# Loading the first tile sooner and doing mixer A's time-step projection during the merge: a two-layer hybrid decoder trunk on eight cores

## The chip, the cores and the metric

The kernel runs on all eight cores of one Trainium2 chip. Each core does one of the eight batch elements, so the cores do the same work and don't talk to each other. The metric is the device time of the slowest core in microseconds (us). A core has five engines that run in parallel: PE (TensorE, matmuls), DVE (VectorE), ACT (ScalarE), POOL (GpSimd) and SP (SyncE). The DMA engines move data and are started from the queues of SP, ACT and POOL.

A program on all eight cores has two states. In the fast one all cores hold nearly the full TensorE clock. In the slow one the cores of one die, or of both, show a lower granted clock in the records. A ratio below is the mean time of one kernel's fast runs over the mean of the other's of the same rounds, so it is not quite the ratio of the medians quoted beside it. Because few runs are wholly fast, I use a second measure too, called the **core mean**: the mean span of all cores that sit on an undisturbed die (granted clock above 0.985), over all runs of a kernel, with its standard error. It takes the mean of the cores where the metric takes the slowest, so it is some 20 us lower; between groups of runs I compare only the differences from the kernel before of the same group.

## The reference

```python
def hybrid_layer(x, pos, c_act, w_ada, b_ada, w_in, ...):      # cut and condensed
    shift, scale, gate = split(c_act @ w_ada + b_ada)          # each (B, 2048)
    h    = x * (1 + scale) + shift
    proj = h @ w_in                                            # one combined projection
    (a_z, a_xbc, a_dt, b_q, ..., merge) = split(proj)
    ys = (ssd_branch(a_z, a_xbc, a_dt, ...),                   # mixer A: Mamba-2
          swa_branch(...), shortconv_branch(...), rglru_branch(...))   # mixers B, C, D
    m   = sum_k sigmoid(merge_k + b_gate_k) * (ys[k] @ w_branch[k])
    return layer_norm(alpha * x + gate * (m @ w_out), ln_w, ln_b)

def ssd_branch(z, xbc, dt, ...):                               # mixer A, cut
    dt  = softplus(dt + dt_bias)                               # (B, L, 16 heads)
    da  = dt * -exp(a_log)
    cum = cumsum(da, within chunks of 128 tokens)              # the cumulated decay
    ...                                                        # exp(cum_l - cum_s) weights the chunk
```

There are 8 batch elements of 2048 tokens, 2048 channels and two layers. The inputs are random, not zeros.

## The kernel before

Each layer is done in two halves of 1024 tokens, and a half as two tiles of 512 (`ti` = 0, 1). A half has a projection and mixer stage (mixers A to D), a merge stage of 16 steps of 41.5 us, an output stage of 16 products, and layer norm. From one half to the next there is a **boundary**; the program has three. Every operation is recorded with a priority `P.key`; a list scheduler then fixes each engine's order, and semaphores are set where one operation needs another.

The head of the program computes the conditioning of the first two thirds (`shift`, `scale`): 32 weight pieces of 1 MB are multiplied by c on DVE. Then x is loaded and h is made from it:

```python
    P.key = -2.0                                     # c: after all the weights
    P.dma("sp", CACT, c_in, writes=[rCACT], nbytes=8192)
    ...
    P.key = -100.0
    for b4 in range(4):
        for blk in (b4, 4 + b4):
            ...
            ada_piece(0, blk, kc, 4, acc_t, slot, "sp" if np_ % 2 == 0 else "act", [rGO] if np_ == 22 else [])
    ...
    P.key = -50.0
    for kc in range(NKC):
        make_h(0, 0, kc, WS1 if kc % 2 else WS2)     # x in the projection weights' buffers
```

While half n is merged, the h of half n+1 is made and stored to HBM, then loaded when the merge is over:

```python
    def pre_h(n, kc):                                # called once per merge step
        w, rw = WS1.get()
        P.dma("sp", xt, src[kc, :, ...], reads=..., writes=[rw], ...)
        for ti in range(NU):
            b, rb = BB.get()                         # 8 buffers of bf16 512
            act(b, xt[...], AF.Identity, ...)        # ScalarE makes h
            P.dma("sp", hs[n, ti][...], b, reads=[rb], writes=[rHS[n][kc]], ...)
            BB.put((b, rb))
        WS1.put((w, rw))
```

At a boundary, mixer A's small "dt chain" is done for each tile of 512 tokens by itself, with that tile's new h:

```python
    def dt_a(l, u, ti):
        pb, rpb = PX.get()                           # PX: three PSUM banks, also mixer A's transposes
        for v in range(4):
            mms([(pb[:, v*16:(v+1)*16], HT[ti][:, kc, v*128:(v+1)*128], WDT[:, kc, :], ...) for kc in range(NKC)], ...)
        tt(dtt, pb[:, 0:64], dt_bias, ALU.add, ...)  # reads the bank: 128x64
        PX.put((pb, rpb))
        softplus(...); ...                           # some ten more operations of 128x64
        mms([... "triu", ... "ones" ...]); ...       # cumulated sums
        act(f[0:16, 0:T], pb[0:16, :], AF.Copy, ...)
        P.dma("act", cumd[s]..., f..., ...)          # the decay to HBM; mixer A reads it back broadcast
```

In mixer A, `P.dma("act", cu, cumd[...].partition_broadcast(128))` is that broadcast read, and the ScalarE operations that use it follow on the same in-order queue.

The softmax here doesn't subtract the row's maximum and nothing guards it: scores larger than these inputs give would overflow.

## Time and profile before

| what | number |
|---|---|
| recorded time, median of 6 runs (lowest to highest) | 6867.13 us (6399.38 to 7307.74) |
| the two fast ones of the six | 6399.38 and 6410.06 us |
| fast mean in the four later groups of runs | 6390.7, 6393.9, 6394.9, 6392.1 us |
| profiled execution: slowest core, mean granted clock | 6409.0 us, 0.990 to 0.992 on all cores |
| dense matmuls start | 172.6 us |
| PE's longest wait at the three boundaries | 16.0, 12.0, 7.5 us |

In all views "PE" without idle time in front of it is the good case: the matmuls set the time, and a microsecond in which PE is idle is a microsecond of the total. What PE waited for is therefore the first thing to read. In a line of a timeline, `ps<-arena` says what was written from what (`ps` is PSUM, the banks that PE writes its products to, `arena` the other on-chip memory), and the bracket gives the idle time before it and what ended it.

### The profile page before, as it was taken

The page shows a single profiled execution, that of the slowest core. Times are in us where ns is not written, and L with a number is a line of the kernel's source. Part 1 is how long each engine was busy: PE and PEld are TensorE (multiplying, and loading weights), DVE is VectorE, ACT ScalarE, POOL GpSimd, SP SyncE. Part 2 cuts the span into 40 slices and gives each one's busy share as a digit, 9 for nine tenths or more (in the row PEclk, how much of TensorE's full clock was granted, in tenths as well). Part 3 has the DMA queues.
Part 4 walks back from the last instruction along what each step waited for, and adds up shares of the span by engine and source line. Part 5 has one row for each costly group of instructions (what it writes and reads, how often), then busy time and mean ns, then how long its engine had stood idle before and what let it go on. Part 6 is the DMA issues. An engine that isn't in the chain of part 4 may idle for free.

```text
span 6409.0 us, 91209 instructions; the slowest of 8 cores (6371.9 to 6409.0 us)
## 1 busy us (share of the span) xinstructions
PE 6062.2 (95%) x31047; PEld 2900.4 (45%) x31644; DVE 3457.1 (54%) x6217; ACT 2193.1 (34%) x4123; POOL 580.9 (9%) x1044
## 2 busy tenths in 40 slices
PE   1999999999999999999999999999999999999998
PEld 0444444444444444444444444444444444444445
DVE  5676664344687665432377776322247766622225
ACT  1555541111355453121135555311114545511113
POOL 0111000000001000000000110000000000000004
PEclk9999999999999999999999999999999999999999
DMA  9877668788687766784579776755557776544445
GB/s 281 128 126 129 123 117 181 153 177 197 137 145 126 120 116 125 172 176 77 127 138 144 120 130 117 159 89 90 90 147 139 137 121 120 112 73 76 77 74 149
DMA packets 281833, 838.53 MB, mean 131 GB/s; under 512 B 35488, under 2 KB 63264, under 8 KB 276768
## 3 DMA queue, kind: packets, MB, share of 16 engines
q0 software_dynamic: 134944, 503.51, 49.2%
q1 hardware_dynamic: 100224, 247.05, 13.2%
q10 hardware_dynamic: 46208, 82.09, 5.7%
q8 instruction: 261, 4.28, 0.3%
q14 instruction: 196, 1.61, 0.1%
HBM read 1264.39 MB, written 65.27 MB: 207 GB/s over the span
## 4 chain that ended last, share of the span: by engine, by line
PE 85%; DMA 7%; issue 2%; ACT 2%; DVE 2%; ACTq 1%; SPq 0%; DVEq 0%; POOL 0%; POOLq 0%
PE ps L486 84%; DMA arena<-cum_scr 2%; ACT arena L458 2%; DMA arena<-x_scr 1%; ACTq L275 1%; DVE arena L462 1%; PE ps L491 1%; DVE arena L466 1%; DMA arena<-arena 1%; DMA arena<-wg 1%; DMA cum_scr<-arena 1%; DMA arena<-w 1%; DMA arena<-w_ada 0%; SPq L275 0%; DMA arena<-cp 0%
## 5 line engine op out<-in xcount | busy, mean ns | idle before, releaser
L486 PE MATMUL ps<-arena 128*128 128x512 bf16 (+6 forms) x30407 | 6038.2, 357 | 291.6 <-DVE arena L466 147.7
L486 PEld LDWEIGHTS ps<-arena 128*128 128x128 bf16 (+3 forms) x31004 | 2846.4, 101 | 3387.5 <-issue 464.4
L466 DVE SCALAR_TENSOR_TENSOR arena<-arena,ps 128x512 f32<-128x512 f32 (+1 forms) x832 | 570.8, 690 | 1718.1 <-PE ps L486 1432.1
L458 ACT ACTIVATE arena<-arena 128x512 f32<-128x512 f32 (+11 forms) x2360 | 1108.0, 518 | 1124.8 <-DVE arena L466 426.0
L462 DVE TENSOR_TENSOR arena<-arena 128x512 f32<-128x512 f32 (+7 forms) x2054 | 1231.0, 618 | 337.7 <-ACT arena L458 158.9
L458 ACT ACTIVATE arena<-ps,arena 128x512 f32<-128x512 f32 x648 | 443.8, 687 | 2166.3 <-PE ps L486 2152.7
L466 DVE SCALAR_TENSOR_TENSOR arena<-arena 128x512 f32<-128x512 f32 (+2 forms) x1281 | 920.6, 734 | 351.5 <-ACT arena L458 208.8
L458 ACT ACTIVATE arena<-ps 128x512 f32<-128x512 f32 (+3 forms) x949 | 535.8, 580 | 813.3 <-PE ps L486 651.6
L275 POOL DMA_DIRECT2D arena<-w x544 | 289.5, 532 | 3185.9 <-PE ps L486 2821.6
L462 DVE TENSOR_TENSOR arena<-ps,arena 128x4 f32<-128x4 f32 (+5 forms) x936 | 330.2, 374 | 234.1 <-PE ps L486 152.1
L275 POOL DMA_DIRECT2D arena<-wg x384 | 204.3, 532 | 2313.8 <-PE ps L486 2312.6
L466 DVE SCALAR_TENSOR_TENSOR arena<-ps,arena 128x512 f32<-128x512 f32 (+3 forms) x153 | 104.1, 680 | 164.2 <-PE ps L486 145.1
L462 DVE TENSOR_TENSOR ps<-ps,arena 128x512 f32<-128x512 f32 (+1 forms) x225 | 148.5, 663 | 13.8 <-DVE arena L466 0.5
L491 PE MATMUL ps<-arena 128*128 128x128 bf16 (+1 forms) x640 | 102.6, 250 | 43.2 <-DVE arena L462 42.0
L491 PEld LDWEIGHTS ps<-arena 128*128 128x128 bf16 (+1 forms) x640 | 64.6, 116 | 108.4 <-issue 62.1
L458 ACT ACT_TABLE_LOAD x64 | 82.1, 1283 | 64.6 <-DMA arena<-c 40.6
L462 DVE TENSOR_TENSOR arena<-arena,ps 128x256 f32<-128x256 f32 (+1 forms) x178 | 78.5, 451 | 31.4 <-PE ps L486 26.7
L1061 DVE TENSOR_TENSOR_SCAN arena<-arena 128x512 f32<-128x512 f32 x64 | 80.9, 1264 | 0.5
L477 DVE RECIPROCAL arena<-arena 128x4 f32<-128x4 f32 (+2 forms) x145 | 69.4, 479 | 16.6 <-ACT arena L458 11.0
L472 DVE TENSOR_SCALAR arena<-arena 128x512 bf16<-128x512 f32 (+6 forms) x211 | 66.7, 334 | 20.8 <-DMA arena<-w_ada 10.7
L1211 POOL TENSOR_TENSOR arena<-arena 128x256 f32<-128x256 f32 (+1 forms) x45 | 41.0, 912 | 82.0 <-ACT arena L458 81.7
L1047 ACT ACT_TABLE_LOAD x32 | 41.1, 1283 | 16.1 <-issue 13.4
(24 smaller groups left out, 127.7 us busy)
## 6 DMA issues: line engine op xcount, KB each, us to landing
arena<-w POOLq DMA_DIRECT2D x544, 512.0 KB, 6.4
arena<-wg POOLq DMA_DIRECT2D x384, 512.0 KB, 6.9
arena<-w_ada SPq DMA_DIRECT2D x128, 512.0 KB, 10.6
arena<-cum_scr ACTq DMA_DIRECT2D x128, 256.0 KB, 6.2
arena<-wo_scr SPq DMA_DIRECT2D x64, 512.0 KB, 4.7
arena<-arena ACTq DMA_DIRECT2D x352, 64.0 KB, 4.9
arena<-w_ada ACTq DMA_DIRECT2D x16, 1024.0 KB, 11.0
arena<-w_ada SPq DMA_DIRECT2D x16, 1024.0 KB, 9.8
```

Source lines behind the costliest of these rows:

```text
L275: eng.dma_start(out=o.fn[0], in_=o.fn[1]).then_inc(s, 16)
L458: P.op("act", lambda e: e.activation(out=out, in_=in_, func=func, **kw), reads, writes, cost=c_act(n) + (0.09 if bias is not None and not ...
L462: P.op(eng, lambda e: e.tensor_tensor(out=out, in0=in0, in1=in1, op=op), reads, writes, cost=c_dve(n * (0.5 if fast else 1.0)), acc=acc)
L466: P.op("dve", lambda e: e.scalar_tensor_tensor(out=out, in0=in0, scalar=scalar, in1=in1, op0=op0, op1=op1), reads, writes, cost=c_dve(n) + ...
L472: return e.tensor_scalar(out=out, in0=in0, scalar1=s1, scalar2=None, op0=op0)
L477: P.op("dve", lambda e: e.reciprocal(out=out, in_=in_), reads, writes, cost=0.1 + n * 6.3e-3)
L486: r = e.matmul(out, lhsT=lhsT, rhs=rhs, start=st, stop=sp_, skip_group_check=True)
L491: P.op("pe", lambda e: e.transpose(out=out, in_=in_, identity=ident), reads, writes, cost=cost, acc=acc)
L1047: r = e.activation(out=cv[:, 0:T], in_=cv[:, 0:T], func=AF.Sqrt, scale=-1.0, bias=ko("quarter"))
L1061: P.op("dve", lambda e, cv=cv, a=a, xs=xs, init=init: e.tensor_tensor_scan(out=cv[:, 0:T], data0=a[:, 0:T], data1=xs[:, 0:T], initial=init ...
L1211: P.op("pool", lambda e, s2=s2, f=f: e.tensor_tensor(out=s2, in0=s2, in1=f, op=ALU.add), [rf, rs2], [rs2], cost=0.16 + n * 2.2e-3)
```

## The change

The intent is to start dense matmuls earlier and to take the dt chain off the boundaries. In the head: c first, all conditioning weights on SyncE's queue and contiguous in HBM, x for the first tile between them in its own buffers, x for the second tile on GpSimd's queue, and two projections before the dt chain. At the boundaries: the dt product is accumulated in the merge stage, block by block of h, and one chain for both tiles follows.

```diff
-    P.key = -2.0
+    P.key = -200.0
     P.dma("sp", CACT, c_in, writes=[rCACT], nbytes=8192)
...
-        P.dma(q, w[:, 0:nk * 512], w_ada[l, blk][:, kc * 512:(kc + nk) * 512], ...)
+        P.dma(q, w[:, 0:nk * 512], w_ada[l, blk, kc // 4][:, (kc % 4) * 512:(kc % 4 + nk) * 512], ...)
...
-    def pre_h(n, kc):
+    def pre_h(n, kc, bank):
...
             act(b, xt[:, ti * T:(ti + 1) * T], AF.Identity, ...)
+            mms([(bank[0][:, (4 * ti + v) * 16:(4 * ti + v + 1) * 16], b[:, v * 128:(v + 1) * 128], WDT[:, kc, :], False,
+                  kc == NKC - 1) for v in range(4)], [rb, rWDT], [bank[1]], 4 * 0.06, acc=True)
             P.dma("sp", hs[n, ti][:, kc * T:(kc + 1) * T], b, ...)
             BB.put((b, rb))
...
+    def dt_chain(l, u, tis, bank, pool):        # the body of the old dt_a, over 128 columns for two tiles
...
-        if u == 0:
+        if n == 0:
             layer_consts(l)
+            load_wdt(l)
+        for col in (A_X, A_Z) if n == 0 else ():
+            wt = load1(WS1, l, col, n)
+            pre[col] = proj(0, wt, PX), PX
+            WS1.put(wt)
-        for ti in range(NU):
+        for ti in range(NU) if n == 0 else ():
             dt_a(l, u, ti)
...
+        if n < 3:                                # before the merge stage
+            bank = PX.get()
+            P.op("dve", lambda e: e.memset(bank[0][:, 0:64 * NU], 0.0), ...)
...
-            sums.append((PX.get(), PX.get() if ti == 0 else PM.get()))
+        sums = [(PX.get(), PX.get()), (PM.get(), PM.get())]
...                                              # after the output stage and layer norm
+        P.key = k0 + UL
+        dt_chain((n + 1) // 2, (n + 1) % 2, list(range(NU)), bank, F2)
+        PX.put(bank)
...
-                ada_piece(0, blk, kc, 4, acc_t, slot, "sp" if np_ % 2 == 0 else "act", [rGO] if np_ == 22 else [])
+                ada_piece(0, blk, kc, 4, acc_t, slot, "sp", rGO if np_ == 29 else [])
...
+        for kc in range(4 * b4, 4 * b4 + 4):     # inside the loop over the four groups of weights
+            x, rx = F.get()
+            P.dma("sp", x[:, 0:T], x_in[kc, :, 0:T], writes=[rx], nbytes=262144)
+            first_h(0, kc, x[:, 0:T], rx)
+            F.put((x, rx))
+    for b4 in range(4):
+        P.key = 20.5 + 10.2 * b4
+        x, rx = ring.get()
+        P.dma("pool", ..., x_in[4 * b4:4 * b4 + 4, :, T:2 * T]..., writes=[rx], nbytes=1048576)
...
-    P.key = -50.0
-    for kc in range(NKC):
-        make_h(0, 0, kc, WS1 if kc % 2 else WS2)
```

## The prediction

> **What bounds the kernel now.** I read the cores first: the eight spans of the profiled execution lie between 6371.9 and 6409.0 us at a granted clock of 0.990 to 0.992 on both dies, so it is an undisturbed, fast one. The six times on record run from 6399 to 7308 us; the two lowest, 6399.38 and 6410.06, agree with each other and with this profile, and the others are slow-state runs. All my numbers, the predicted time too, are for the fast state, with 6405 us (the mean of those two) as "before".
>
> Then the page. Busy time with its share and instruction count, and the strips in 40 slices of 160 us:
>
> ```profile
> PE 6062.2 (95%) x31047; PEld 2900.4 (45%) x31644; DVE 3457.1 (54%) x6217; ACT 2193.1 (34%) x4123; POOL 580.9 (9%) x1044
> ...
> PE   1999999999999999999999999999999999999998
> ...
> DMA  9877668788687766784579776755557776544445
> ```
>
> PE is the bound everywhere but in the first slice, where the DMA engines are. All there is to win without removing matmuls is PE's idle time, 6409 - 6062 = 347 us, and this change removes no large matmul. So I asked who PE waited for (total us, times, longest):
>
> ```profile
> PE ps L486 <- DVE arena L466: 147.7, 13, 64.4
> PE ps L486 <- DVE arena L462: 58.1, 45, 5.0
> PE ps L491 <- DVE arena L462: 42.0, 8, 16.0
> ```
>
> The first line is the head; L491 is the transpose of mixer A, of which single waits reach 16 us. I looked at each place in turn. The head by windows (PE, PEld, DVE, ACT, POOL busy; granted clock; DMA share; GB/s):
>
> ```profile
> 0.00:40.00 40.00, 0.00 (x0) 0.00 (x0) 0.12 (x3) 0.00 (x0) 3.83 (x8) 1.00 0.92 283
> 40.00:80.00 40.00, 3.54 (x16) 3.48 (x16) 33.88 (x76) 8.01 (x15) 0.00 (x0) 1.00 0.76 252
> 80.00:120.00 40.00, 3.68 (x16) 3.56 (x16) 24.91 (x46) 5.76 (x8) 0.00 (x0) 1.00 0.97 321
> 120.00:160.00 40.00, 13.52 (x56) 8.85 (x58) 33.45 (x53) 5.76 (x8) 2.13 (x4) 1.00 0.98 268
> 160.00:200.00 40.00, 36.06 (x225) 17.90 (x227) 17.81 (x45) 15.70 (x30) 5.83 (x11) 0.96 0.82 131
> ```
>
> and by the timeline:
>
> ```profile
> 18.49 3.31 SPq L275 DMA_DIRECT2D arena<-c  x1
> ...
> 40.56 1.28 ACT L458 ACT_TABLE_LOAD   x1 [40.56 <-DMA arena<-c]
> ...
> 138.49 0.54 POOL L275 DMA_DIRECT2D arena<-w  x1 [133.81 <-ACT arena L458]
> ...
> 172.59 17.64 PE L486 MATMUL ps<-arena 128*128 128x512 bf16 x77 [0.23 <-issue]
> ```
>
> The 8 KB tensor c, which every conditioning product needs, is issued at 18.5 us behind ten megabytes of weights and x, and lands at 40.6: VectorE does nothing until then. Meanwhile its weight ring is full, so the DMA share falls to 0.76 in the next window. The first projection weight is issued at 138.5 us, because its buffers carry x until ScalarE has made h. Dense matmuls begin at 172.6.
>
> The other place is the boundary from one half of a layer to the next. The chain that ended last, near the first of them:
>
> ```profile
> 1731.11 8.65 DMA cum_scr<-arena
> ...
> 1740.23 18.95 DMA arena<-cum_scr
> ```
>
> and PE's timeline there:
>
> ```profile
> 1763.60 0.59 PE L491 MATMUL ps<-arena 128*128 128x128 bf16 x4 [15.99 <-DVE arena L462]
> 1763.98 3.62 PE L486 MATMUL ps<-arena 128*128 128x512 bf16 x8
> ```
>
> The dt chain of mixer A (small matmuls, about twenty tiny vector operations, a write of the cumulated decay to HBM, a broadcast read of it) only starts when the new h is there; ScalarE waits for the read at the head of its queue, then DVE, then PE, for 16.0 us. At the second boundary the same wait is 12.0 us, at the third 7.5.
>
> **What the Trainium skill says.** (1) "DMA: Bandwidth & Descriptors", Specifications, gives about 358 GB/s of HBM to a core. The trace agrees in kind: 321 GB/s over 80 to 120 us at a share of 0.97. The head is a bandwidth problem, and only bytes moved out of it or idle DMA time can shorten it. (2) Same page, Queues, rings and completion order: an SDMA engine takes its queue rows in turn, packet by packet. So weights on GpSimd's queue will take a share from conditioning weights still under way on SyncE's. No view before isolates this. (3) "TensorE: Matmul & The Clock Gate", Part 1: the array falls to half clock when idle for a window of about 3.4 us and takes about as long to recover. The trace agrees: the 8 matmuls after the 16 us gap took 3.62 us, 452 ns each, where dense ones take about 217, and the clock over 1700 to 1760 us is 0.93.
>
> **The change part by part.** *Head.* c and the constants get the lowest key, so they go first; the adaptive weights all go on SyncE's queue, each piece contiguous in HBM; x for the first 512 tokens is loaded between them as 256 KB tiles; x for the second 512 follows on GpSimd's queue after the first projection weights. Projection weights wait for piece 29 of 32 (counted from 0) and find all eight buffers free. (The three "go" resources are written by that same transfer, so they gate alike.)
>
> Before: prior to the dense start PE had done 35 + 20 + 11 matmuls of 512 columns, 14 us at full clock, and 1.8 us for dt. Its effective start is 172.6 - 16 = 156.6 us.
>
> After: the bytes ahead of the last h of the first 512 tokens are 32 x 1.049 = 33.6 MB and 16 x 0.262 = 4.2 MB, 37.8 MB in all, at 321 GB/s 118 us, and about 3 us to start. The last three megabytes (two pieces and the last x tiles) share with projection weights, by the skill's second point half and half: 3.1 MB of delay, 10 us. So the data is there at 131. The end chain before, from the last DVE products at 158.1 to the first h at 166, took 8 us; I take 7: h at 138. DVE needs 32 x 4 x 0.67 = 86 us and is not the bound. By 138 some 43.3 - 37.8 = 5.5 MB, five weight tiles, have landed, and on three quarters of the h PE can have done 4 x 12 matmuls, 10.4 us. Afterwards weights come at 1.049 / 0.321 = 3.3 us a tile and a tile feeds 16 x 0.217 = 3.5 us of one 512-token projection, so the late x (4.2 MB, 13 us) isn't hidden: less the 9 us of work in stock, 4 us of starvation, and 2 us of cold clock. Effective start 138 - 10.4 + 6 = 133.6. Gain 23 us.
>
> *Boundaries.* The dt projection moves into the preceding merge stage as 4 small matmuls per h block, accumulating in a zeroed bank. The number of dt matmuls is unchanged (64 took 1.81 us), so in a stage where PE is busy 39.8 of 40 us they cost what they save. The rest of the dt chain is done for 1024 tokens at once in the output stage, where DVE is busy only 25 of 40 us. About 25 operations of some 0.2 us vanish per boundary, 5 us of DVE, which is not the bound. The chain's write of 8.65 us leaves the path; the broadcast read does not, since its buffers overlay what the output matmuls read until the boundary. PE had 17 us of work from the write's issue to the gap; with only the 19 us read left, 2 to 3 us of the 16 remain. I allow 7 us left over of 35.5 for all three: 28. The cold clock after a gap costs 3.62 - 1.73 = 1.9 us; three, 6. Together 34.
>
> *Banks.* The output stage has three PSUM banks for products, not four. A product takes 16 x 0.217 = 3.5 us and its eviction about 0.75, so two would do: 0. The second layer's constants leave the boundary: DVE only, 0.
>
> Sum: 23 + 34 = 57 us of 6405, so 6348.
>
> **The rivals.** *A new wait takes the old one's place.* DVE is busy 34.4 of 40 us before the first boundary and 30 to 35 after it, and ScalarE still blocks on the broadcast read, at a DMA share of 0.84 to 1.03. For it: the next chunks also wait for such reads (1884.8, 12.65 us) with dt long done. Against it: at 1748 to 1763 DVE itself waits. It leaves half the boundary gain: 6365. *The head's transfers collide.* If weights and late x starve PE for 15 us more, the head gives 8: 6363; if the contiguous pieces run at the 340 to 350 GB/s of the best slices, it gives 30: 6341. *The merge pays.* The dt matmuls wait for h blocks whose x is late; ScalarE waits for x 12 times, up to 6.4 us, in the first merge and up to 16.8 us in the third. They stand behind the block's own matmuls, with some 40 us of slack, so I expect nothing; 1 us in each of 48 blocks would eat nearly all: 6396. *All goes well:* no gaps, 30 us at the head, and the A chain pulls in later waits: 6315.
>
> **Range and chances.** 6348 us, 8 in 10 between 6312 and 6385. Over 2% faster means below 6277, 128 us off: more than the head and all three gaps can give together without removing matmuls, so 0.04. Slower by 2% would need 185 us of new waits, only if the order of issue misfits the chip badly: 0.02. Within 2%: 0.94.
>
> **What would show it.** c landing within 5 us, DVE starting below 10; a DMA share above 0.95 to 105 us; the first projection weight at 105 to 115; dense matmuls from about 138; no L491 wait over 4 us at a boundary, the decay written to HBM 50 us or more before it; unchanged merges of about 660 us. I am wrong if dense work starts after 155, if ScalarE still waits 15 us for the broadcast with PE idle behind it, or if merge or output stages grow by over 5 us each.

## More of the kernel before

A buffer comes from a pool and goes back to its end. Recording order therefore decides which earlier user a new user of a buffer waits for.

A few per cent of matmul records can be missing from a trace (core 2 of before has 31047 matmuls for 31644 weight loads), so PE's busy totals are not compared between single cores. On before, the two cores with missing records have idle sums of 347 and 323 us, the other six 282 to 303 us.

For the experiments I summed PE's idle time per stretch of the program from the matmul records, as the mean of the undisturbed cores of the profiled run: 144.0 us in the first 300 us of the kernel before, 22.5, 16.3 and 13.1 us in the 230 us after each of the three boundaries, and 64.0 us in the rest of the second, third and fourth halves up to their output stages.

## The result

The changed kernel gives correct results. Its nine recorded runs have a median of 6629.67 us (6326.34 to 7416.99), those of the kernel before beside it a median of 6799.09 us (6392.27 to 7508.14, 18 runs). The ratio of fast runs is **0.9893, with a 95% interval of 0.9877 to 0.991**, so the time is 1.1% lower. Applied to the 6405 us of the prediction this is 6336 us; the fast runs lie between 6324.28 and 6341.33 us. The recorded profile of the changed kernel fell in the slow state (die 0 with a median of 7018.4 us at clock 0.879, die 1 with 6306.9 us at 0.996), so the kernel was run again (label after_again), and the profile of that fast run is read here. Its eight cores have spans from 6303.8 to 6323.4 us at a clock of 0.995 or 0.996.

The page of the changed kernel, core 5, the slowest: busy time, then the strips of PE and of the DMA engines in 40 slices.

```profile
PE 6085.3 (96%) x31632; PEld 2897.7 (46%) x31632; DVE 3459.6 (55%) x6154; ACT 2193.8 (35%) x4118; POOL 580.9 (9%) x1048
...
PE   2999999999999999999999999999999999999998
...
DMA  9877768788797666775578776556558766544445
```

The first slice of PE rises from 1 to 2 tenths; the rest looks alike, and DVE has 63 instructions fewer and is no less busy. The waits of PE on the same core say more (total us, times, longest):

```profile
PE ps L486 <- DVE arena L466: 126.6, 14, 25.5
PE ps L486 <- DVE arena L462: 55.5, 45, 5.1
PE ps L486 <- ACT arena L458: 18.3, 14, 3.6
...
PE ps L491 <- DVE arena L466: 3.5, 2, 2.0
PE ps L491 <- DVE arena L462: 2.6, 1, 2.6
```

The head's line falls from 147.7 to 126.6 us, and the longest wait in it from 64.4 to 25.5. Of the transposes' 42.0 us in eight waits, 2.6 and 3.5 are left. The line for ScalarE has a counterpart in before (core 2), the next after the three that the prediction shows:

```profile
PE ps L486 <- ACT arena L458: 35.0, 17, 13.4
```

The head by windows (PE, PEld, DVE, ACT and POOL busy; granted clock; DMA share; GB/s), and two lines of its timeline (start, duration, engine, line, operation):

```profile
0.00:40.00 40.00, 1.84 (x8) 1.78 (x8) 22.96 (x63) 2.57 (x7) 3.82 (x8) 1.00 0.92 288
40.00:80.00 40.00, 5.52 (x24) 5.35 (x24) 32.53 (x49) 5.66 (x8) 0.00 (x0) 1.00 0.99 342
80.00:120.00 40.00, 5.45 (x24) 5.35 (x24) 32.73 (x49) 3.13 (x5) 1.53 (x2) 1.00 1.00 340
120.00:160.00 40.00, 23.97 (x161) 12.70 (x161) 18.87 (x45) 16.24 (x27) 7.38 (x13) 1.00 1.02 220
160.00:200.00 40.00, 39.99 (x243) 18.85 (x241) 19.99 (x39) 16.95 (x36) 4.24 (x8) 1.00 0.83 127
```

```profile
1.07 0.38 SPq L275 DMA_DIRECT2D arena<-c  x1
...
137.93 73.03 PE L486 MATMUL ps<-arena 128*128 128x16 bf16 x448 [3.60 <-ACT arena L458]
```

The tensor c is issued at 1.07 us instead of 18.49, the DMA share stays at 0.99 and more from 40 to 160 us, and dense matmuls begin at 137.93 us (139.8 as the mean of the eight cores). From there PE has 448 matmuls in 73 us without a gap that the view would split off. The dt products (128x16) still come first, although the projections are recorded ahead of them; the first projection matmul follows at 141.6 us (mean). The first boundary (PE and the queue of ScalarE, core 5):

```profile
1692.51 0.33 ACTq L275 DMA_DIRECT2D cum_scr<-arena  x1
...
1696.98 0.36 ACTq L275 DMA_DIRECT2D arena<-cum_scr  x1
...
1715.25 0.39 PE L491 MATMUL ps<-arena 128*128 128x128 bf16 x4
1715.48 27.79 PE L486 MATMUL ps<-arena 128*128 128x512 bf16 x128
```

The four transposes that waited 16.0 us on core 2 of before, and 11.4 on its core 5, now wait for nothing. The decay is written at 1692.5 us, though, and read back 4.5 us later: that is 1.3 us after VectorE starts its last layer-norm sum of the output stage, not 50 us ahead of the boundary.

The idle sums put the whole gain in three places (us, mean of the undisturbed cores of each profiled run):

| stretch | before | changed | difference |
|---|---|---|---|
| head, 0 to 300 us | 144.0 | 130.4 | -13.6 |
| 230 us after the boundaries | 22.5 + 16.3 + 13.1 | 9.8 + 2.6 + 6.1 | -33.4 |
| rest of halves two to four, up to their output stages | 64.0 | 49.8 | -14.2 |
| sum | 259.9 | 198.7 | -61.2 |
| core mean | 6370.9 ± 2.1 | 6307.8 ± 2.9 | -63.1 |

That the sum and the core mean agree so well is partly chance. The two profiled runs themselves lie 76.6 us apart (mean spans of 6387.2 and 6310.6 us), as that of before is slower than the core mean of its kernel. Over the whole span idle time fell by 64.5 us (303.2 to 238.7) and PE's busy time by 12.1. The records of the granted clock account for the second part: PE was busy at half clock, after gaps, for so long that 33.3 us were lost before and 21.5 us after. So some five sixths of the gain are idle time, and most of the rest is a clock that falls less often. One profiled run stands for each kernel: those kernels below that keep the boundaries of before have 41.7 to 48.1 us in the second row, so some of the 33.4 us is spread between runs. The third row is the surprise: nothing in the change was meant for it.

### The profile page after: what moved, and what is told of

It reads as the page before. It is cut to its first block, busy times and chain, and to the rows that moved or that the text cites. A ratio compares the mean times of both kernels' runs of the same rounds, so it can differ in the third digit from the quotient of the medians.

```text
span 7024.7 us, 91720 instructions; the slowest of 8 cores (6291.3 to 7024.7 us)
## 1 busy us (share of the span) xinstructions
PE 6830.3 (97%) x31632; PEld 3088.2 (44%) x31632; DVE 3468.2 (49%) x6154; ACT 2201.2 (31%) x4118; POOL 583.3 (8%) x1048
## 4 chain that ended last, share of the span: by engine, by line
PE 92%; DMA 3%; DVE 2%; ACT 1%; issue 1%; ACTq 1%; SPq 0%; DVEq 0%; POOL 0%; POOLq 0%
PE ps L486 91%; DMA arena<-w_ada 1%; ACT arena L458 1%; PE ps L491 1%; DVE arena L466 1%; DMA arena<-cum_scr 1%; ACTq L275 1%; DVE arena L462 1%; DMA arena<-arena 1%; DMA arena<-wg 0%; SPq L275 0%; DMA arena<-x 0%; ACT L458 0%; DVEq L263 0%; DVE arena L472 0%
## 5 line engine op out<-in xcount | busy, mean ns | idle before, releaser
L486 PE MATMUL ps<-arena 128*128 128x512 bf16 (+6 forms) x30992 | 6804.6, 387 | 173.1 <-DVE arena L466 126.1
L486 PEld LDWEIGHTS ps<-arena 128*128 128x128 bf16 (+2 forms) x30992 | 3031.7, 107 | 3843.4 <-issue 2654.7
L458 ACT ACTIVATE arena<-arena 128x512 f32<-128x512 f32 (+8 forms) x2354 | 1103.7, 519 | 1099.3 <-DVE arena L466 488.0
L466 DVE SCALAR_TENSOR_TENSOR arena<-arena 128x512 f32<-128x512 f32 (+1 forms) x1278 | 926.1, 735 | 360.1 <-ACT arena L458 217.7
L458 ACT ACTIVATE arena<-ps 128x512 f32<-128x512 f32 (+5 forms) x946 | 536.9, 581 | 1079.9 <-PE ps L486 928.1
L462 DVE TENSOR_TENSOR arena<-ps,arena 128x256 bf16<-128x256 f32 (+6 forms) x930 | 329.6, 376 | 362.4 <-PE ps L486 246.9
L462 DVE TENSOR_TENSOR ps<-ps,arena 128x512 f32<-128x512 f32 (+1 forms) x225 | 148.0, 663 | 13.6 <-DVE arena L466 0.9
L477 DVE RECIPROCAL arena<-arena 128x4 f32<-128x4 f32 (+2 forms) x145 | 69.4, 479 | 19.7 <-ACT arena L458 14.2
```

Source lines behind the costliest of these rows:

```text
L458: P.op("act", lambda e: e.activation(out=out, in_=in_, func=func, **kw), reads, writes, cost=c_act(n) + (0.09 if bias is not None and not ...
L462: P.op(eng, lambda e: e.tensor_tensor(out=out, in0=in0, in1=in1, op=op), reads, writes, cost=c_dve(n * (0.5 if fast else 1.0)), acc=acc)
L466: P.op("dve", lambda e: e.scalar_tensor_tensor(out=out, in0=in0, scalar=scalar, in1=in1, op0=op0, op1=op1), reads, writes, cost=c_dve(n) + ...
L477: P.op("dve", lambda e: e.reciprocal(out=out, in_=in_), reads, writes, cost=0.1 + n * 6.3e-3)
L486: r = e.matmul(out, lhsT=lhsT, rhs=rhs, start=st, stop=sp_, skip_group_check=True)
```

## The experiments

The runs came in four groups; each group shares its runs of the kernel before, whose core means are 6370.9, 6373.4, 6382.4 and 6371.4 us (± 1.4 to 2.1). All kernels gave correct results. Theory at the outset: the head gives some 15 us, and the boundaries the rest because the chain's start and its write lie earlier. Rival: the chain's earliness is worth little, and the gain is from something else that goes with the dt part.

### The two halves of the change: head_only, dt_only, and the changed kernel again

after_again is the changed kernel. head_only is the kernel before with the hunks of the head alone, dt_only with those of the dt product, the chain and the banks alone.

> The changed kernel once more, for a profile in the fast state. Ratio to before 0.987 to 0.992 (some 65 us). On a fast core: PE's first dense matmul near 138 us, no wait of PE at a boundary over 5 us, the decay written to HBM only in the last 10 us of each output stage.

> Only the head part of the change; the dt chain stays at the boundaries. Theory (parts add up): 15 to 25 us faster than before, ratio 0.996 to 0.9975, with the boundary waits of 8 to 16 us still there. Rival (the gain comes from the new order as a whole, the parts do not add): under 8 us or over 35 us.

> Only the dt part of the change; the head is as before, dense matmuls begin near 172 us. Theory: 34 to 50 us faster than before, ratio 0.992 to 0.995, no boundary wait over 5 us. Rival (the chain is hidden by other work, the gap comes from the broadcast read): under 15 us.

| kernel | ratio of fast runs [95%] | fast mean, runs | core mean | idle: head, boundaries, rest |
|---|---|---|---|---|
| after_again | 0.9897 [0.9875, 0.9919] | 6324.9, 4 | 6307.8 ± 2.9 | 130.4, 18.5, 49.8 |
| head_only | 0.9982 [0.9956, 1.0009] | 6379.8, 3 | 6355.8 ± 1.6 | 130.3, 41.7, 61.1 |
| dt_only | 0.9915 [0.9891, 0.9938] | 6336.1, 3 | 6326.1 ± 1.5 | 145.2, 19.0, 48.2 |

The parts add up. By the slowest core the head gives 11 us (0.0018 of 6390.7; its interval touches 1) and the dt part 54; by the core mean 15 ± 3 and 45 ± 3. dt_only leaves the idle time of the head as it was. head_only has 10 us less at the boundaries than before, though, which nothing in it explains; c_first, c_first_sp and paced below, with the same boundaries, have 48.1, 46.1 and 46.3, so I take it as the spread between profiled runs, and the parts are studied apart. The head is less than was predicted, and the dt part more.

### The head: c_first, c_first_sp

Which part of the head counts? c_first only issues c and the constants ahead of the weights; c_first_sp puts all the conditioning weights on SyncE's queue too.

```diff
# c_first (from before)
-    P.key = -2.0
+    P.key = -200.0
     P.dma("sp", CACT, c_in, writes=[rCACT], nbytes=8192)
# c_first_sp: this, and
-                ada_piece(0, blk, kc, 4, acc_t, slot, "sp" if np_ % 2 == 0 else "act", ...)
+                ada_piece(0, blk, kc, 4, acc_t, slot, "sp", ...)
```

> The kernel before with one line changed: c, the constants and both parameter tables are loaded first. Theory (the DMA engines idle some 13 us of the head because VectorE waits for c): VectorE starts before 12 us, dense matmuls begin 8 to 14 us earlier than 172.6, total 8 to 14 us faster (ratio 0.998 to 0.9988). Rival (weights for the projections gate the start, they wait for buffers that carry x): dense start moves by less than 4 us and the time does not change.

> The kernel before with c and the tables first, and all adaptive weight pieces on SyncE's queue instead of every second one on ScalarE's. c first alone changed nothing, though VectorE started 30 us earlier: its DMA share was still 0.86 and 0.85 in two of the first four windows. Theory (pieces on ScalarE's queue wait behind its making of h): share above 0.95 in all windows from 40 to 160 us, last h 6 to 12 us earlier than 168, ratio 0.997 to 0.999. Rival (the two x halves are what counts, all bytes must come before the last h): last h moves by under 4 us.

c_first measured 1.0003 [0.9983, 1.0024], core mean 6368.0 ± 2.9 (2.9 less than before, within its error). The windows of its slowest core, and one line of its PE timeline, show what an early c does by itself:

```profile
40.00:80.00 40.00, 2.78 (x13) 2.66 (x14) 20.22 (x31) 5.75 (x8) 0.00 (x0) 1.00 0.86 286
...
120.00:160.00 40.00, 15.19 (x59) 8.43 (x61) 24.29 (x36) 5.75 (x8) 2.13 (x4) 1.00 0.85 240
```

```profile
168.57 13.00 PE L486 MATMUL ps<-arena 128*128 128x16 bf16 x114 [0.75 <-ACT arena L458]
```

VectorE starts its products of weights 21 us sooner (21.7 for 42.7 us, means of eight cores), but the first matmul that needs all of h starts only 5.6 us sooner (164.9 for 170.5; 168.6 on this core). The hole in the DMA share did not go on this core; 0.86 and 0.85 are left in these two windows. With ScalarE's queue freed, c_first_sp measured 0.9985 [0.9971, 1.0], core mean 6366.0 ± 1.7 against 6373.4. Its theory did not come true: the share is 0.99 in the windows from 40 to 120 us but 0.67 from 120 to 160 (core 3), and the first matmul that needs all of h comes at 163.4 us, 1.5 us before that of c_first. The idle time of the head is 144.0 before, 137.4 in c_first, 134.3 in c_first_sp and 130.3 in head_only: the gain is made of small steps, and none of them is the part that counts. The start of dense matmuls is not the measure either: head_only has it at 140.8 us, 22.6 us before c_first_sp, and yet only 4.0 us less idle time, since c_first_sp, like before, does some 60 matmuls of the projections ahead of that point and head_only none.

### The layout of the conditioning weights: strided, strided_2

From the changed kernel, the old layout, in which a partition's row is 32 KB from the next and a piece takes 8 KB of it.

```diff
-        ... w_ada[l, blk, kc // 4][:, (kc % 4) * 512:(kc % 4 + nk) * 512] ...
+        ... w_ada[l, blk][:, kc * 512:(kc + nk) * 512] ...
```

> The changed kernel with the old layout of the adaptive weights (rows 32 KB apart in HBM instead of contiguous pieces). Theory (the layout is worth nothing; the pieces come at 320 to 340 GB/s both ways): same time as the changed kernel within 4 us, first h at 136 to 140 us. Rival (the contiguous layout raised the rate from 321 to 337 GB/s): first h 5 us later or more.

> The changed kernel with the strided layout, once more. Its first reading had two fast runs and lay some 10 us over the changed kernel with the same head. Theory (the layout is worth nothing): within 4 us of the control. Rival (it costs later, in the adaptive pieces loaded during the merges): 8 us or more slower.

strided had two fast runs (6346.37 and 6329.02), too few for an interval, and a core mean of 6321.6 ± 3.4, which looked like a loss of some 10 us. The repeat, beside a control run of the changed kernel, took that back: fast runs 6325.38 and 6323.52, core mean 6310.4 ± 1.7 against 6310.6 ± 2.3 of the control. The layout is worth nothing here. The first reading was chance, and it shows how little two fast runs and a comparison across groups can carry.

### The order of late x and first weights: x_after_w

In the changed kernel the second tile's x is issued on GpSimd's queue at 116.0, 119.5 and 123.3 us (core 6), ahead of the first projection weights at 124.0. x_after_w holds it back until the weights may go.

```diff
         P.dma("pool", ..., x_in[4 * b4:4 * b4 + 4, :, T:2 * T]...,
-              writes=[rx], nbytes=1048576)
+              reads=[rGO[0]], writes=[rx], nbytes=1048576)
```

> The changed kernel, where the x of the second 512 tokens also waits for weight piece 29, so that it follows six projection weights on GpSimd's queue instead of going ahead of them. Theory (the late x takes half the rate from the last pieces): first h 4 to 7 us earlier than 137.6, 3 to 8 us faster than the changed kernel, ratio 0.988 to 0.989. Rival (then the projection weights take that half, and PE starves for x later): first h unchanged within 2 us or new waits of PE between 140 and 240 us, no gain.

The first weight was issued at 122.3 instead of 125.1 us and landed at 130.0 instead of 138.4, and the first matmul of the projections ran at 137.9 instead of 141.6 (means of eight cores). There was one fast run, 6323.58. The core mean, 6311.5 ± 2.0, is 70.9 us below before of its group; for the changed kernel it is 63.1 and, in a repeat, 60.8. That would be 8 to 10 us, with an error of some 4 between groups, but the kernel `best` below, which has this edit too, shows nothing of it. No gain can be claimed.

### Is it the chain's early start? late_chain, early_cum, early_cum_2

late_chain makes the first operation of the wide chain read the layer-norm statistics too, so that the chain can't start before the output stage is over. early_cum goes the other way and gives the chain the priority of the output stage's beginning.

```diff
# late_chain (from after)
-        tt(dtt, pb[...], dt_bias, ALU.add, [rpb, rCP[l]], rd, n=n)
+        tt(dtt, pb[...], dt_bias, ALU.add, [rpb, rCP[l], rRSTD[1]], rd, n=n)      # at the three boundaries
# early_cum (from after)
-        P.key = k0 + UL
+        P.key = k0 + SM
         dt_chain((n + 1) // 2, (n + 1) % 2, list(range(NU)), bank, F2)
```

> The changed kernel, where the first step of the wide dt chain also reads the layer norm's row of the second token tile, so that the chain starts only after the output stage; the moved dt matmuls, the wide operations and the banks stay. Theory (it is the start of the chain that closes the gaps): 25 to 45 us of the dt part's 45 to 55 are lost, ratio 0.994 to 0.997, and waits of 8 us or more are back at the boundaries. Rival (fewer vector operations or the moved matmuls do it): under 10 us lost.

> The changed kernel with the chain's priority raised, so that its last matmuls go between the output products and the decay is written some 80 us before the boundary, as I had predicted and as the changed kernel does not do. Theory (the broadcast read can't be issued before the output matmuls let go of its buffers, so the write is hidden already): same time as the changed kernel within 5 us. Rival (the write's 5 to 9 us still are on the path at three boundaries): 10 to 25 us faster than the changed kernel, ratio 0.986 to 0.988.

late_chain measured 0.9918 [0.9903, 0.9934] and a core mean of 6322.0 ± 3.5. It gives back only 0.0021 of 6391, 13 us, of the change's gain (12 us by core means, each against before in its own group, with an error of some 5; the two intervals overlap). This is nearer to the rival's size than to the theory's. Its decay is written 42 us after the start of the last layer-norm sum of the output stage, even later than in before (36 to 38 us), as the queue of ScalarE (core 6) and PE's waits around the first boundary show:

```profile
1722.20 0.33 ACTq L275 DMA_DIRECT2D cum_scr<-arena  x1
```

```profile
PE ps L486 <- DVE arena L462: 13.1, 4, 4.6
```

Instead of one wait of 16 us there are four, the longest 4.6, and the transposes don't wait. **So the theory falls for most of the gain:** the early start is worth some 12 us of the dt part's 45 to 54, and the rest comes with something else that the dt part does.

early_cum measured 0.9884 [0.9866, 0.9902], core mean 6299.5 ± 1.6. It was repeated with a control:

> Control: the changed kernel on the same chip. Ratio 0.989 to 0.9905.

> The changed kernel with the chain's priority raised, once more. If its first reading (0.9884) was real: 5 to 12 us faster than the control. If it was chance: within 3 us.

after_3, the changed kernel once more, has 0.9906 [0.9888, 0.9923] and 6310.6 ± 2.3; early_cum_2 has 0.9884 [0.9865, 0.9904] and 6302.1 ± 2.4. It is ahead of the changed kernel both times, by 8 and 14 us of the fast runs and by 11 and 8.5 ± 3.3 us of the core means, so it beats both kernels, by little. It doesn't do so by what I expected, a write some 80 us ahead. On core 6 of early_cum_2, where the output stage's last sum starts at 1703.8 us, the queue of ScalarE has

```profile
1701.40 0.33 ACTq L275 DMA_DIRECT2D cum_scr<-arena  x1
...
1706.19 0.94 ACTq L275 DMA_DIRECT2D arena<-cum_scr  x2
```

Absolute times of a boundary differ by some microseconds from core to core, so I take them from the start of VectorE's last layer-norm sum in the output stage (means of the eight cores). In early_cum the write comes 2.4 us before it, at all three boundaries, where the changed kernel has it 1.3 to 6.4 us after; the read comes 2.4 us after it, where the changed kernel has 5.8 to 11. The chain's VectorE operations do run during the output stage in the changed kernel (128x128 operations from 1581 us on, core 6). What holds the write back after that I have only read from the code: the last small matmuls have a lower priority than the output products, and the copy's buffer is the next in a pool that those products use. No run tests it.

### Is it the PSUM bank? dt1_after, late_rot

In before, every one of the long waits of the transposes ends as VectorE reads the dt products of the second tile. The timeline of before, core 2, at the second boundary:

```profile
3342.11 0.22 DVE L462 TENSOR_TENSOR arena<-ps,arena 128x64 f32<-128x64 f32 x1
...
3342.48 0.58 PE L491 MATMUL ps<-arena 128*128 128x128 bf16 x4 [11.97 <-DVE arena L462]
```

The 128x64 operation reads the bank that the transposes get next, because banks rotate in the order of recording and the second tile's chain is recorded before mixer A. The operation itself stands on VectorE behind work that waits for ScalarE, which waits for the broadcast read. The same pair is at 1763.23 and 1763.60 us and at 4896.38 and 4896.74, and all eight cores have it at each boundary, 0.37 us apart. New theory: this hold, which the change removes by using one bank, is what counts. dt1_after removes it alone, by recording the second tile's chain after the first tile's mixer; late_rot puts it back into late_chain.

```diff
# dt1_after (from before)
         for ti in range(NU):
             P.key = k0 + 60.0 * ti
             dt_a(l, u, ti)
-        for ti in range(NU):
             mix_a(l, n, ti, ...)
# late_rot (from late_chain): the chain's bank goes back to the pool ahead of the sums' banks
-        PX.put(*sums[0])
-        PM.put(*sums[1])
         P.key = k0 + UL
         dt_chain(...)
         PX.put(bank)
+        PX.put(*sums[0])
+        PM.put(*sums[1])
```

> The kernel before with one change: the dt chain of the second token tile is written after mixer A of the first, so that the first transposes of mixer A take a PSUM bank that the second tile's dt products do not hold. In the kernel before, each long wait of these transposes ends 0.15 us after DVE reads the second tile's dt products out of that bank. Theory (the bank rotation makes the gap; the broadcast read only holds DVE up): the four-transposes waits of 6 to 16 us vanish, 20 to 35 us faster than before, ratio 0.9945 to 0.997. Rival (the read and the chain's latency make the gap): PE still waits 6 us or more at each boundary, under 8 us gained.

> The kernel with the late chain, where the chain's bank is handed back first, so that the first transposes of the next mixer A take it and wait until the chain is done. Theory (bank rotation): gaps of 5 to 12 us are back at the boundaries, 8 to 25 us slower than the late chain alone, ratio 0.993 to 0.996. Rival (fewer operations and the moved matmuls gain the rest): as the late chain, 0.9918 within 0.001.

dt1_after measured 1.0001 [0.9964, 1.0039], core mean 6376.5 ± 3.5 against 6382.4: no gain that can be told from nothing. Its PE and ScalarE queue on core 1:

```profile
1719.46 0.39 PE L491 MATMUL ps<-arena 128*128 128x128 bf16 x4
...
1734.44 0.33 ACTq L275 DMA_DIRECT2D cum_scr<-arena  x1
...
1763.15 0.45 PE L491 MATMUL ps<-arena 128*128 128x128 f32 x1 [11.51 <-DVE arena L466]
```

The bf16 transposes don't wait any more, so the bank was what held them. But PE then stands 11.5 us at the f32 transposes, 44 us further on, behind the same broadcast read. The idle time of the boundaries falls by 16.7 us (to 16.3 + 10.7 + 8.2; other kernels with the boundaries of before lie 4 to 10 us under it as well), while that of 230 to 400 us after them rises from 3.6 to 14.8 us in all: the wait is moved, not removed. The bank is the place where PE was stopped, and not what most of the time was lost to. late_rot measured 0.9929 [0.988, 0.9977] and 6333.8 ± 3.3; against late_chain that is 7 to 9 us more by fast runs and some 3 by the core means, each set against its own before. The boundaries' idle time rises from 30.3 to 37.9 us, which is no more than the spread between profiled runs. Whether the bank costs something beside the rest is inconclusive.

### All that seemed good together: best

```diff
# from after
-        P.key = k0 + UL
+        P.key = k0 + SM          # as in early_cum
         dt_chain(...)
-              writes=[rx], nbytes=1048576)
+              reads=[rGO[0]], writes=[rx], nbytes=1048576)      # as in x_after_w
```

> The raised priority of the chain (which gave 0.9884) and the x after the weights together. If both gains hold and add up: 8 to 15 us faster than the changed kernel, ratio 0.987 to 0.9885. If they do not, not under 0.9884.

There was one fast run, 6330.94, and a core mean of 6313.6 ± 2.3: not better than early_cum alone, which agrees with x_after_w having nothing to add.

### The third merge stage: paced

14 us of idle time vanish outside head and boundaries, also in dt_only and late_chain (48.2 and 46.1 for 64.0), but not in dt1_after (71.7). They lie mainly at the start of the third merge stage, where before has 17.5 us of idle time and the changed kernel 6.5. There the two traces differ in when the h blocks of the next half are stored. The view of the tile h_scr on core 2 of before, with the number of stores, the shortest, median and longest issue in ns, and the first and last start in us; and PE's longest waits from 3900 to 4200 us:

```profile
L275 SPq DMA_DIRECT2D h_scr<-arena x32: 319/320/2713, 4042.0 to 4124.8; - x32
```

```profile
PE ps L486 <- ACT arena L458: 15.5, 3, 13.4
```

and the stores of the changed kernel, core 2:

```profile
L275 SPq DMA_DIRECT2D h_scr<-arena x32: 319/319/815, 3977.2 to 4479.7; - x32
```

Before makes all 16 blocks of h in a burst of 83 us; nothing but priority paces them. The loads of x then pile up, ScalarE stands at the head of its queue with an activation whose x is not there, and PE waits up to 13.4 us for ScalarE operations that stand behind it in the same queue. In the changed kernel a block's eight bf16 buffers are held until the dt products have read them, and these products stand in PE's order among the merge steps, so the stores come over 502 us. That the buffers do the pacing is read from the code and these times. Theory: this pacing is the unexplained gain. paced does that alone in before, by making the load of a block wait for the merge step four earlier.

```diff
# paced (from before)
         P.dma("sp", xt, src[kc, :, ...], reads=([rX1[t0 + i][kc] for i in range(NU)] if l else [])
+              + ([rMT[1][kc - 4]] if kc > 3 else []),
               writes=[rw], nbytes=262144 * NU)
```

> The kernel before, where the load of x for the h block dc of the next half also waits for the merged block dc-4, so that the h blocks come one per merged block instead of in a burst of 16 within 80 to 300 us; nothing of the change is in it. Theory (the burst makes ScalarE wait at the head of its queue for x, and PE behind it): PE's idle time in the merges of the second and third half falls by 10 to 18 us, 8 to 22 us faster than before, ratio 0.9965 to 0.9987, the boundary gaps stay. Rival (the merges gain from something else): idle time there unchanged, ratio 0.999 or more.

paced measured 0.9972 [0.9938, 1.0007] by two fast runs and a core mean of 6352.3 ± 2.0 against 6371.4 ± 1.4: 19.1 ± 2.4 us less. Its interval of fast runs still touches 1; I rest on the core mean and on the trace. On core 2:

```profile
L275 SPq DMA_DIRECT2D h_scr<-arena x32: 319/319/556, 4019.1 to 4530.5; - x32
```

```profile
PE ps L486 <- ACT arena L458: 1.5, 1, 1.5
```

The burst is gone, and of PE's 15.5 us in this window 1.5 are left; the changed kernel has 2.4. The idle time outside head and boundaries falls from 64.0 to 46.3 us, to the level of every kernel with the dt part, and that of the head stays (144.5). So the burst costs this time in before, and pacing alone removes it. That the changed kernel gains the same through the accidental pacing by its buffers agrees with its trace, but no run takes the pacing out of it, and paced was not repeated.

### What remains open

Of the dt part's 45 us (core mean), pacing is about 19 and the early start some 12, if these add up. The remaining 13 or so, itself with an error of some 6, came already in late_chain: one wide chain instead of two narrow ones, no dt products at the boundary, and the bank. No run separates them, beyond late_rot's 3 to 9 us for the bank.

## Why the prediction was right or wrong

The number for the fast state was near: 6348 us, where the fast-state value is 6336. For the recorded median, 6629.67 us, it was far too low. "All my numbers, the predicted time too, are for the fast state" leaves the slow state out, though four of the six runs given for before were slow; so were five of the nine of the changed kernel. In the sum itself the step that failed is the path at the boundaries, "The chain's write of 8.65 us leaves the path": the write came 1.3 to 6.4 us after the start of the output stage's last sum, and giving up the chain's early start cost only some 12 of the dt part's 45 us. With it failed the overlap of the first projections with the loading of the head, and the zero for the merges, where pacing alone gained some 19 us (paced). The sum was near partly by luck, as terms missed in opposite directions.

- *Where the bound is.* Right. In the pair of profiled runs idle time is 64.5 of the 76.6 us that went; 11.8 are clock lost while PE is busy, of which the working had 6, at the boundaries (6.5 measured there). The 347 us of idle time were read on a core with missing records; the complete cores have 282 to 303.
- *Head, 23 us.* Mis-sized: 15 by the core mean, 11 by the slowest core, 13.6 of idle time. First h at 138 and dense matmuls from then on were right (137.93 us on core 5, 139.8 in the mean, where the first matmul that needs all of h came at 170.5 before). What failed is the term "on three quarters of the h PE can have done 4 x 12 matmuls, 10.4 us": none of it happened before 138, because the first weight was issued at 125.1 us, not 105 to 115, and landed at 138.4. Piece 29, for which the weights wait, landed at 120.1, and late x went ahead of them on the same queue; without that (x_after_w) the first weight landed at 130.0. On the other hand PE hardly starved afterwards (0.5 us idle up to 210 us and 2.5 up to 240, where I took 6 of starvation and cold clock). The 10.4 us were lost and some of the 6 won back. The DMA rate, which I took as 321 GB/s, was 340 to 342.
- *Boundaries, 34 us.* The size was near: 28 us of idle time and 6 of cold clock were forecast, and 33.4 and 6.5 went in the pair of profiled runs, with several us of spread. The mechanism was half right. "The chain's write of 8.65 us leaves the path" and "the decay written to HBM 50 us or more before it" were false, as said above. Moving the chain back behind the boundary (late_chain) cost only some 12. The chain's lateness thus explains about a third of it.
- *Merges, 0 us.* Failed. The rival had the very wait in sight, "up to 16.8 us in the third", and set it aside with "some 40 us of slack, so I expect nothing". The products did cost nothing; but loads that are paced, as holding the h buffers until then does, are worth about 19 us by paced, which nothing in the working had. I had read that wait only as a threat to the change, not as a loss that the kernel already had; and the answer on PE's waits that the prediction quotes goes on with ScalarE at 35.0 us and 13.4 at the longest, which it did not follow up.
- *Banks, 0 us.* Not shown to be wrong. The hold of a bank was where the 16.0 us were spent, which the working missed, but taking it away alone gained nothing that could be told from zero.
- *The rivals.* That the broadcast read would take the write's place and leave half of the boundary's gain did not happen; that the head gives less than hoped did, for another reason: weights that came late, not weights that starved PE after the start.

## What to carry to other kernels

A wait in a profile shows where an engine was stopped, and the bank experiment shows that removing the stop alone can simply move the wait 44 us on; ask what the releaser itself was waiting for. When work is fed ahead by priority alone, look whether it arrives in a burst: tying it to the progress of the consumer gained 19 us here with one line, about as much as the whole reordering of the head (15). And before crediting a gain to what a change was meant to do, put that one thing back: here that left most of the gain standing.

## What the Trainium skill lacked or had wrong

- "TensorE: Matmul & The Clock Gate", Part 1 (the caution on the peak-current limiter) says that once three cores of a die run dense matmuls the whole die goes to 13/16 of the clock and stays there under load, and advises to budget for it. Here eight cores with PE busy 95 to 96% and random inputs hold a mean granted clock of 0.990 to 0.996 in the fast runs; only some executions of the same kernel show a die lowered, to means of 0.877 to 0.881 in the recorded profile. The page lacks that there are two states.
- "DMA: Bandwidth & Descriptors", Latency and other measured facts, advises to lay tiles out contiguously or to pad, with losses measured at row pitches of 512 KiB and more. It has no figure for small pitches: at 32 KB the strided and the contiguous layout gave 6310.4 ± 1.7 and 6310.6 ± 2.3 us.
- I found no page that says that work fed ahead by priority alone can stall the in-order queue of ScalarE and through it PE. Here it cost waits of up to 13.4 us, and pacing it gained 19.1 ± 2.4 us.
- Nor one that says that recording order, through the rotation of PSUM banks, can make a product wait for a read which stands far behind on another engine. Here it was the place of waits of 16.0, 12.0 and 7.5 us.
